# A per-token factor in a delta-rule scan: from a second copy of y on ACT to a copy of the keys on POOL

## The chip, the cores and the metric

One core of a Trainium2 chip runs the whole kernel in one launch. The metric is the device time of that core in microseconds, the median of several runs. The engines that matter here are PE (matrix products), DVE and ACT (vector work that may read the matrix products' memory, PSUM), POOL (vector work that reads and writes SBUF only) and SP, which issues the DMAs. Each engine works through its own queue in order; an instruction that must wait holds up everything behind it on its engine.

## What is computed

One encoder layer: a normalisation, one projection whose columns feed two head groups, and an output projection. Group B is windowed attention. Group A, where the change lies, is a gated delta rule, run forward and backward over the sequence, in chunks. The kernel uses chunks of 128 tokens where the reference uses 64. Cut to the step that is touched, the reference is:

```python
def step(state, inp):
    q_i, k_i, u_i, w_i, g_i, a_i = inp
    v_new = u_i - jnp.einsum('bhcd,bhde->bhce', w_i, state)
    o = (jnp.einsum('bhcd,bhde->bhce', q_i * jnp.exp(g_i)[..., None], state)
         + jnp.einsum('bhcs,bhse->bhce', a_i, v_new))
    g_last = g_i[..., -1]
    k_dec = k_i * jnp.exp(g_last[..., None] - g_i)[..., None]
    state = state * jnp.exp(g_last)[..., None, None] + jnp.einsum('bhcd,bhce->bhde', k_dec, v_new)
    return state, o
```

The state product sums over the tokens of a chunk. The factor exp(g_last - g) belongs to a token, so it may stand on the keys (as above) or on v_new: the sum is the same.

## The kernel before

Four heads, 16 chunks of 128 tokens each, two directions. From about 775 us on, the four heads' scans follow each other. Inside `scan(h, H)` a loop runs over 16 steps and, in each, over the two directions d; their states are independent of each other. One step and direction is: `pk` = the chunk's keys times the state (PE, L847); `r` from it on DVE (L849); `py` = the inverted triangular matrix times r (PE, L856); `yk` and `y`, two copies of py from PSUM to SBUF on ACT, the first with the per-token factor `ck` (L861, L863); the state product `po[:, 0]` of the keys `ks` and yk (PE, L865); the new state `S` on DVE (L868); and the outputs `po[:, 1]` and `po[:, 2]` (PE, L874, L858), which are put together in `oacc` on ACT and DVE (L881 to L885). The last step makes no new state, so 120 of the 128 chunk steps have a yk.

While head h is scanned, later heads are prepared. `pre_front` reads keys, queries and values, transposes them (`tr`, `trv`), squares and sums the keys on ACT (`jk`, L716, whose sums are `ssk`), adds the decay mask on POOL (`v_q` and `dc`, L699), takes a square root on POOL (`nk`, L718), scales the values by it on ACT (`vs`, L749) and makes the products `gh` (L728) and `ma` (L737). `solve` inverts small diagonal blocks on DVE, 31 columns one after the other (L775, L779). `invert` reads these back (`xc`, transposed `xt`), places them in `iv` and `ma` with copies on DVE and POOL (L802, L819) and builds the full inverse with products `pi` on PE (L807). As filling work PE also takes the attention group's share of the output projection, units of twelve products `pcs` (L622 to L624) with their splits `mhs` and `mls`. A unit takes a PSUM bank that `trv` or `gh` uses too, so it cannot begin before `vs` has read trv. At a scan's end `post` normalises and transposes the outputs (`jko`, `sso`, `tro`).

The order on each engine is not the program's. `set_order` builds the graph of dependencies with estimated durations, plans a queue for each engine, and then moves single instructions or short runs of them by a table of numbers, `TURNS`, one string for each engine.

Of the kernel before, what the change touches and what calls it, by code (L numbers as in the profile page):

```python
# [7 lines left out]
F32 = mybir.dt.float32  # L8
F32R = mybir.dt.float32r
AF = mybir.ActivationFunctionType  # L10
ALU = mybir.AluOpType
# [4 lines left out]
P = 128  # L16
# [556 lines left out]
def phase_b(ctx, wide, xe, ae, late, tc, t, ident, consts, hp, mix_dn, mix_sw, kq_d, v_d, zdn_d, zsw_d, dp, out):  # L573
# [259 lines left out]
    def scan(h, H):  # L833
# [3 lines left out]
        for i in range(NCH):  # L837
            for d in range(2):
# [20 lines left out]
                if i < NCH - 1:  # L859
                    yk = rp.tile([P, P], F32, tag="yk", name=f"yk{nm}", bufs=3)  # L860
                    A.activation(yk, py, AF.Copy, scale=ck[:, d, c : c + 1])  # L861
                y = rp.tile([P, P], F32, tag="y", name=f"y{nm}", bufs=3)
                A.activation(y, py, AF.Copy)  # L863
                if i < NCH - 1:
                    T.matmul(po[:, 0], ks[c4][:, cl], yk, start=True, stop=True)  # L865
                    s_new = rp.tile([P, P], F32, tag=f"S{d}", name=f"S{nm}", bufs=3)
                    if i:
                        V.scalar_tensor_tensor(  # L868
                            s_new, st[d], egt[:, d, c, h : h + 1], po[:, 0], ALU.mult, ALU.add
                        )  # L870
                    else:
                        V.tensor_copy(s_new, po[:, 0])
                    st[d] = s_new
# [185 lines left out]
    for c, e in zip(ORD[::2], ORD[1::2]):  # L1059
# [37 lines left out]
    ),  # L1097
    "DVE": (
# [455 lines left out]
```

## Time and profile before

| what | value |
|---|---|
| median of 3 runs | 1241.33 us (1239.07 to 1242.42) |
| the profiled execution | 1243.42 us, its span 1241.2 us |
| PE busy | 1206.3 us, 97% of the span |
| DVE busy | 945.5 us, 76% |
| ACT busy | 728.2 us, 59% |
| POOL busy | 524.5 us, 42% |
| chain that ended last | PE 82%, DVE 8%, DMA 4%, POOL 2%, ACT 2%, issue 2% |

The span runs from the first to the last instruction; 2.2 us of the profiled execution lie outside it. Matrix products overlap in their pipeline, so "busy" is an upper value of PE's work. Idle time of PE is what another order or a faster neighbour can give back.

### The profile page before, as it was taken

To read this page: it belongs to the slowest core of one execution; us is meant where nothing else is said; L and a number is where in the kernel's file an instruction comes from. 1 tells how busy PE (TensorE), PEld (TensorE's weight loads), DVE (VectorE), ACT (ScalarE), POOL (GpSimd) and SP (SyncE) were. 2 spreads that over 40 slices of the span, in tenths; PEclk is the share of its full clock that TensorE was granted. 3 is DMA by queue.
4 is the path that set the end of the run, shared out by engine and by line. 5 is a ranking of instruction groups with operands and counts; after the bars stand their busy time and mean duration, and the time that the engine had idled before them with its cause. 6 is when DMAs were issued, how large, how long until landed. Compare 5 with 4: busy or idle time off the path is not lost.

```text
span 1241.2 us, 22493 instructions
## 1 busy us (share of the span) xinstructions
PE 1206.3 (97%) x7080; PEld 1041.0 (84%) x7080; DVE 945.5 (76%) x2325; ACT 728.2 (59%) x2169; POOL 524.5 (42%) x845
## 2 busy tenths in 40 slices
PE   9999999999999999999999999899899899999998
PEld 9998888888889988887878877798689689888787
DVE  5523689999854369999997577799779989866765
ACT  6432476766634357776666546758566855686421
POOL 2243454754202185656532203704652461670442
PEclk9999999999999999999999999999899999999999
DMA  7653242523354434430115857967965875853785
GB/s 233 203 152 126 78 157 74 197 65 103 103 195 148 139 110 153 132 103 31 65 48 168 258 160 228 262 211 210 260 184 169 255 218 161 244 187 107 250 281 207
DMA packets 232295, 205.87 MB, mean 166 GB/s; under 512 B 49137, under 2 KB 181873, under 8 KB 232178
## 3 DMA queue, kind: packets, MB, share of 16 engines
q1 hardware_dynamic: 232178, 204.45, 53.4%
q8 instruction: 56, 0.92, 0.3%
q14 instruction: 61, 0.50, 0.1%
HBM read 139.32 MB, written 65.08 MB: 165 GB/s over the span
## 4 chain that ended last, share of the span: by engine, by line
PE 82%; DVE 8%; DMA 4%; POOL 2%; ACT 2%; issue 2%; SPq 0%; POOLq 0%; ACTq 0%; DVEq 0%
PE pf_c L224 7%; PE pf_c L223 7%; PE pf_c L225 7%; PE pf_z L223 4%; PE pf_z L224 4%; PE pf_z L225 4%; PE pi L807 4%; PE pt L416 3%; PE pq_q L238 2%; PE pq_q L237 2%; PE pq_q L236 2%; PE py L856 2%; PE pcd L1021 2%; PE pcd L1020 2%; PE pcd L1022 2%; PE pcs L622 2%
## 5 line engine op out<-in xcount | busy, mean ns | idle before, releaser
L223 PE MATMUL pf_c<-xhi,wh_c 128*128 128x512 f32 x384 | 155.0, 404 | 0.0
L224 PE MATMUL pf_c<-xlo,wh_c 128*128 128x512 f32 x384 | 154.4, 403 | 0.0
L225 PE MATMUL pf_c<-xhi,wl_c 128*128 128x512 f32 x384 | 153.9, 401 | 0.0
L295 DVE SCALAR_TENSOR_TENSOR acc<-pf_c,cw,acc 128x512 f32<-128x512 f32 (+1 forms) x192 | 141.1, 743 | 4.1 <-ACT acc L291 1.7
L411 POOL TENSOR_SCALAR pr<-pr,st 128x384 f32<-128x384 f32 (+1 forms) x128 | 76.4, 616 | 108.4 <-DVE st L409 72.8
L420 ACT ACTIVATE ph<-pt 128x512 fp32r<-128x512 f32 x92 | 53.1, 596 | 61.3 <-PE pt L416 54.4
L402 ACT ACTIVATE pr<-pr,st 128x384 f32<-128x384 f32 (+1 forms) x128 | 76.1, 596 | 16.0 <-DVE st L398 15.7
L225 PEld LDWEIGHTS pf_c<-xhi,wl_c 128*128 128x128 f32 x384 | 72.2, 188 | 13.2
L223 PEld LDWEIGHTS pf_c<-xhi,wh_c 128*128 128x128 f32 x384 | 72.4, 188 | 12.2
L224 PEld LDWEIGHTS pf_c<-xlo,wh_c 128*128 128x128 f32 x384 | 72.3, 188 | 12.1
L861 ACT ACTIVATE yk<-py,ck 128x128 f32<-128x128 f32 x120 | 44.0, 367 | 58.5 <-PE py L856 57.0
L398 DVE CUSTOM_DVE_ANT_0 pr<-s,mask,sink 128x384 f32<-128x384 f32 (+1 forms) x128 | 74.0, 595 | 3.6 <-PE pt L416 1.7
L237 PE MATMUL pq_q<-wh_q,xlo 128*128 128x256 f32 x256 | 72.1, 282 | 0.0
L238 PE MATMUL pq_q<-wl_q,xhi 128*128 128x256 f32 x256 | 71.9, 281 | 0.0
L236 PE MATMUL pq_q<-wh_q,xhi 128*128 128x256 f32 x256 | 71.4, 280 | 0.0
L416 PE MATMUL pt<-ident,pr 128*128 128x128 f32 x368 | 67.4, 273 | 1.1 <-DVE q L380 0.5
L718 POOL TENSOR_TENSOR nk<-ssk,pw 128x4 f32<-128x4 f32 x16 | 16.6, 1035 | 119.5 <-DVE ssk L717 119.5
L421 DVE TENSOR_TENSOR pl<-pt,ph 128x512 fp32r<-128x512 f32 x92 | 61.6, 683 | 6.0 <-ACT ph L420 5.4
L622 PE MATMUL pcs<-wohs,mhs 128*128 128x512 f32 x128 | 57.4, 449 | 5.4 <-ACT mhs L616 1.9
L416 PEld LDWEIGHTS pt<-ident,pr 128*128 128x128 f32 x368 | 48.1, 140 | 16.9 <-POOL pr L411 2.4
L623 PE MATMUL pcs<-wohs,mls 128*128 128x512 f32 x128 | 55.4, 433 | 0.5 <-DVE mls L617 0.5
L624 PE MATMUL pcs<-wols,mhs 128*128 128x512 f32 x128 | 54.3, 424 | 0.2 <-DVE wols L600 0.2
(336 smaller groups left out, 4017.3 us busy)
## 6 DMA issues: line engine op xcount, KB each, us to landing
kqc<-kq_d SPq DMA_DIRECT2D x120, 128.0 KB, 3.0
ws_c<-wt SPq DMA_DIRECT2D x48, 256.0 KB, 3.5
k_q<-kq_d SPq DMA_DIRECT2D x16, 512.0 KB, 5.1
mxs<-mix_sw SPq DMA_DIRECT2D x32, 256.0 KB, 3.3
xrs<-x SPq DMA_DIRECT2D x32, 256.0 KB, 3.6
part<-xrs SPq DMA_DIRECT2D x32, 256.0 KB, 2.5
xrd<-part SPq DMA_DIRECT2D x32, 256.0 KB, 3.5
out<-xrd SPq DMA_DIRECT2D x32, 256.0 KB, 2.3
```

What stands on the lines that cost most here:

```text
L223: T.matmul(ps, hi[:, k, cs], xhi[b][:, k], start=(k == 0), stop=False)
L224: T.matmul(ps, hi[:, k, cs], xlo[b][:, k], start=False, stop=False)
L225: T.matmul(ps, lo[:, k, cs], xhi[b][:, k], start=False, stop=(k == KC - 1))
L236: T.matmul(ps[:, :n], xh, hi[:, k, :n], start=(k == 0), stop=False)
L237: T.matmul(ps[:, :n], xl, hi[:, k, :n], start=False, stop=False)
L238: T.matmul(ps[:, :n], xh, lo[:, k, :n], start=False, stop=(k == KC - 1))
L295: V.scalar_tensor_tensor(av, ps[:, lo:], cw[:, i, k : k + 1], av, ALU.mult, ALU.add)
L398: V.tensor_tensor_reduce(pr[j][:, :n], ps[:, :n], mask[:, lo * P : hi * P], 1.0, sink[:, hh : hh + 1], ALU.add, ALU.min, accum_out=nm[:, j ...
L402: A.activation(pr[j][:, :n], pr[j][:, :n], AF.Exp, bias=nm[:, j : j + 1], scale=-1.0, accum_out=den[:, j : j + 1])
L411: G.tensor_scalar(pr[j][:, :n], pr[j][:, :n], den[:, j : j + 1], 1.0, ALU.mult, ALU.mult)
L416: T.transpose(pt[:, j], pr[j][:, (kb - lo) * P : (kb - lo + 1) * P], ident)
L622: T.matmul(ps, mh[:, k], wh[:, k], start=(k == 0), stop=False)
```

## The change

The copy yk is gone. In its place POOL writes `kd`, the keys times the same factor ck, into a ring of three buffers, and the state product takes kd and the plain copy y. kd needs nothing that the running step makes: keys and factors are ready before the scan starts. Its buffer comes free when the state product three before it has read it.

```diff
@@ scan
                 if i < NCH - 1:
-                    yk = rp.tile([P, P], F32, tag="yk", name=f"yk{nm}", bufs=3)
-                    A.activation(yk, py, AF.Copy, scale=ck[:, d, c : c + 1])
+                    kd = rp.tile([P, P], F32, tag="yk", name=f"kd{nm}", bufs=3)
+                    G.tensor_scalar(kd, ks[c4][:, cl], ck[:, d, c : c + 1], None, ALU.mult)
                 y = rp.tile([P, P], F32, tag="y", name=f"y{nm}", bufs=3)
                 A.activation(y, py, AF.Copy)
                 if i < NCH - 1:
-                    T.matmul(po[:, 0], ks[c4][:, cl], yk, start=True, stop=True)
+                    T.matmul(po[:, 0], kd, y, start=True, stop=True)
@@ TURNS: all five strings are replaced, for example the end of Pool's
-        "1,2 1,4 -5 4,12 1 -2 1,5 1 -2 1 1 -2 1,5 1 -2 4 -4,3 1,13 1,4 -5 4,4"
+        "-3,2 1,37 1 -2 1,6 1 -2 1 4 -5,4 1,6"
```

The graph has other instructions now, so the planned queues differ as well as the table, on every engine and in every stage. Three places matter below. In a name such as yk1_0_2 the numbers are head, direction and step; in nk2 and v2_q the digit is the head and the buffer; dc2_3_1 is head 2, quarter 3; the last number is the tile's own.

On ACT, at the start of head 1's scan, the queue was:

```order
L816 ACTIVATE b11_1_10511<-pi0_1_1_10506 128x512
L861 ACTIVATE yk1_0_0_10688<-py1_0_0_10685,ck1_9822 128x128
L863 ACTIVATE y1_0_0_10690<-py1_0_0_10685 128x128
L736 ACTIVATE v2_q_7777<-v2_q_7777,ngc_4962 128x128
L861 ACTIVATE yk1_1_0_10701<-py1_1_0_10698,ck1_9822 128x128
L863 ACTIVATE y1_1_0_10703<-py1_1_0_10698 128x128
```

With the change the same place reads:

```order
L863 ACTIVATE y1_0_0_10690<-py1_0_0_10685 128x128
L816 ACTIVATE b11_1_10511<-pi0_1_1_10506 128x512
L863 ACTIVATE y1_1_0_10703<-py1_1_0_10698 128x128
L879 ACTIVATE oacc1_0_10696<-po1_0_0_10686 128x128
L879 ACTIVATE oacc1_3_10709<-po1_1_0_10699 128x128
L863 ACTIVATE y1_0_1_10723<-py1_0_1_10717 128x128
L736 ACTIVATE v2_q_7777<-v2_q_7777,ngc_4962 128x128 x3
```

Two rows of yk are gone, and the decay mask's exponentials (L736, on v2_q) stand behind the third y where one stood between the first and the second pair.

On POOL, at the end of head 0's scan, the last quarter of head 2's preparation stood so before:

```order
L699 TENSOR_TENSOR v2_q_7777<-v2_q_7777,dmask_4923 128x512 x2
L718 TENSOR_TENSOR nk2_11396<-ssk2_11395,pw_4931 128x4
L795 TENSOR_TENSOR g1_1_10492<-xhi_h_9090 128x512
L699 TENSOR_TENSOR v2_q_7777<-v2_q_7777,dmask_4923 128x512
L718 TENSOR_TENSOR nk2_11396<-ssk2_11395,pw_4931 128x4
L699 TENSOR_TENSOR dc2_3_1_11627<-dc2_3_1_11627,dmask_4923 128x512
L613 TENSOR_TENSOR mxs9_0_11722<-mxs9_0_11722,zcs9_0_11724 128x512
```

and now so, with the first copies of head 1's keys among it:

```order
L699 TENSOR_TENSOR v2_q_7777<-v2_q_7777,dmask_4923 128x512 x2
L613 TENSOR_TENSOR mxs9_0_11722<-mxs9_0_11722,zcs9_0_11724 128x512
L718 TENSOR_TENSOR nk2_11396<-ssk2_11395,pw_4931 128x4
L861 TENSOR_SCALAR kd0_1_14_9732<-ks0_0_7947,ck0_7806 128x128
L861 TENSOR_SCALAR kd1_0_0_10688<-ks1_0_9978,ck1_9822 128x128
L861 TENSOR_SCALAR kd1_1_0_10701<-ks1_3_10051,ck1_9822 128x128
L861 TENSOR_SCALAR kd1_0_1_10721<-ks1_0_9978,ck1_9822 128x128
L718 TENSOR_TENSOR nk2_11396<-ssk2_11395,pw_4931 128x4
L699 TENSOR_TENSOR v2_q_7777<-v2_q_7777,dmask_4923 128x512
L699 TENSOR_TENSOR dc2_3_1_11627<-dc2_3_1_11627,dmask_4923 128x512
```

The last nk2 stood behind a v2_q row before and stands ahead of it now; four kd rows are ahead of it.

On POOL, at the end of head 1's scan, the rows of head 3's preparation were:

```order
L718 TENSOR_TENSOR nk3_12986<-ssk3_12985,pw_4931 128x4
L699 TENSOR_TENSOR v2_q_7777<-v2_q_7777,dmask_4923 128x512 x2
L718 TENSOR_TENSOR nk3_12986<-ssk3_12985,pw_4931 128x4 x2
L699 TENSOR_TENSOR v2_q_7777<-v2_q_7777,dmask_4923 128x512
L819 COPY ma2_0_11553<-xt2_0_0_12008 32x4x32 x2
```

and are now:

```order
L699 TENSOR_TENSOR v2_q_7777<-v2_q_7777,dmask_4923 128x512 x2
L718 TENSOR_TENSOR nk3_12986<-ssk3_12985,pw_4931 128x4
L861 TENSOR_SCALAR kd2_0_0_12278<-ks2_0_11562,ck2_11399 128x128
L861 TENSOR_SCALAR kd2_1_0_12291<-ks2_3_11635,ck2_11399 128x128
L861 TENSOR_SCALAR kd2_0_1_12311<-ks2_0_11562,ck2_11399 128x128
L699 TENSOR_TENSOR v2_q_7777<-v2_q_7777,dmask_4923 128x512
L718 TENSOR_TENSOR nk3_12986<-ssk3_12985,pw_4931 128x4
L699 TENSOR_TENSOR dc3_3_1_13212<-dc3_3_1_13212,dmask_4923 128x512
```

Here the last nk3 stood ahead of the third v2_q row and now stands behind it and behind three kd rows.

## Rows read from the trace of the kernel before

**Rows 1.** The page, parts 1 and 2: PE busy; its granted clock in 40 slices (tenths).

```profile
PE 1206.3 (97%) x7080; PEld 1041.0 (84%) x7080; DVE 945.5 (76%) x2325; ACT 728.2 (59%) x2169; POOL 524.5 (42%) x845
PEclk9999999999999999999999999999899999999999
```

**Rows 2.** Stretches: length, busy PE, PEld, DVE, ACT, POOL (instructions), clock, DMA share, GB/s.

```profile
868.00:899.00 31.00, 24.82 (x129) 21.00 (x129) 22.48 (x67) 17.78 (x74) 17.96 (x37) 0.83 0.90 255
961.00:992.00 31.00, 25.37 (x161) 20.88 (x161) 28.00 (x95) 27.75 (x136) 11.90 (x16) 1.00 0.89 262
775.00:1155.00 380.00, 356.59 (x2473) 318.91 (x2472) 313.65 (x949) 258.29 (x959) 164.83 (x287) 0.99 0.70 206
```

**Rows 3.** Waits of PE, 775 to 1155: total us, times, longest us.

```profile
PE po L865 <- ACT yk L861: 1.9, 4, 1.2
PE pcs L622 <- ACT mhs L616: 1.9, 2, 1.2
PE pcs L622 <- ACT vs L749: 1.9, 1, 1.9
...
PE trv L745 <- ACT jk L716: 1.6, 3, 0.8
PE pcs L622 <- ACT wohs L599: 1.5, 2, 0.9
```

**Rows 4.** Groups of ACT, 775 to 1155: count, busy us, mean ns, idle before.

```profile
L861 ACT ACTIVATE yk<-py,ck 128x128 f32<-128x128 f32 x120 | 44.0, 367 | 58.5 <-PE py L856 57.0
L863 ACT ACTIVATE y<-py 128x128 f32<-128x128 f32 x127 | 34.6, 272 | 1.8 <-PE py L856 1.7
```

**Rows 5.** Two POOL operations by line: ns least/median/most, shapes.

```profile
L109 POOL TENSOR_SCALAR sink<-sink x1: 259/259/259, 27.9 to 27.9; 128x8 f32<-128x8 f32 x1
L411 POOL TENSOR_SCALAR pr<-pr,st x128: 472/589/1616, 143.6 to 663.8; 128x384 f32<-128x384 f32 x112, 128x256 f32<-128x256 f32 x16
```

**Rows 6.** Timeline of ACT, start of head 1's scan: start, us, row, [idle before].

```profile
902.52 0.40 ACT L736 ACTIVATE v_q<-v_q,ngc 128x128 f32<-128x128 f32 x1 [1.98 <-POOL v_q L699]
902.83 0.35 ACT L861 ACTIVATE yk<-py,ck 128x128 f32<-128x128 f32 x1
```

**Rows 7.** Timeline of PE at the same place.

```profile
903.23 0.49 PE L865 MATMUL po<-yk,ks 128*128 128x128 f32 x2 [1.22 <-ACT yk L861]
```

**Rows 8.** Timeline of POOL at the end of head 0's scan.

```profile
873.21 1.27 POOL L699 TENSOR_TENSOR v_q<-v_q,dmask 128x512 f32<-128x512 f32 x1 [6.86 <-DMA v_q<-gr_d]
874.43 1.02 POOL L718 TENSOR_TENSOR nk<-ssk,pw 128x4 f32<-128x4 f32 x1
```

**Rows 9.** Timeline of PE at the same place, into head 1's inversion.

```profile
876.68 0.50 PE L622 MATMUL pcs<-wohs,mhs 128*128 128x512 f32 x1 [1.87 <-ACT vs L749]
...
884.17 1.91 PE L807 MATMUL pi<-iv,g 128*128 128x128 f32 x8 [2.00 <-DVE iv L802]
```

**Rows 10.** Stretches at the same place, columns as in the stretches above.

```profile
876.00:882.00 6.00, 5.32 (x16) 4.07 (x16) 3.52 (x11) 4.72 (x21) 3.99 (x10) 0.72 1.01 275
882.00:886.00 4.00, 2.00 (x9) 1.64 (x8) 3.80 (x16) 1.20 (x9) 0.73 (x2) 0.79 1.05 296
886.00:892.00 6.00, 5.31 (x25) 4.88 (x25) 4.17 (x14) 3.69 (x11) 4.34 (x12) 0.57 0.75 212
```

**Rows 11.** Timeline of POOL at the end of head 1's scan.

```profile
982.77 1.01 POOL L718 TENSOR_TENSOR nk<-ssk,pw 128x4 f32<-128x4 f32 x1 [5.38 <-DVE ssk L717]
983.74 1.27 POOL L699 TENSOR_TENSOR v_q<-v_q,dmask 128x512 f32<-128x512 f32 x1
```

**Rows 12.** Timeline of POOL and DVE inside head 0's scan.

```profile
844.06 1.28 POOL L613 TENSOR_TENSOR mxs<-mxs,zcs 128x512 f32<-128x512 f32 x1
...
844.62 0.95 DVE L779 TENSOR_TENSOR X<-X,tm 128x207 f32<-128x207 f32 x1
```

**Rows 13.** Groups of DVE, 775 to 1155: the two products of the solve.

```profile
L775 DVE TENSOR_TENSOR tm<-L,X 128x31 f32<-128x31 f32 (+15 forms) x93 | 34.2, 368 | 2.3 <-POOL X L770 1.4
L779 DVE TENSOR_TENSOR X<-X,tm 128x31 f32<-128x31 f32 (+15 forms) x93 | 34.0, 365 | 0.7
```

138 rows, old and new, of the table TURNS are left out of this document.

## Prediction, made before the changed kernel ran

> **What bounds the kernel now.** I read the page first, for where engines are busy and where PE's clock falls. PE is busy 97% of the span, and its granted clock is full in every slice but one, near 880 us [rows 1]. So the kernel is worth about what PE must do, and a change can win only where PE stands still or runs at the lower clock. The view of busy time by stretch then says where that is. In the scans, 775 to 1155 us, PE is busy 356.6 of 380 us, so it is idle for 23.4; 6.2 of these lie in 868 to 899 and 5.6 in 961 to 992, which are the ends of head 0's and head 1's scans [rows 2]. The change touches no instruction outside the scans except by order, so these 23.4 us are the field.
>
> Next, who ends PE's waits there [rows 3]. ACT is named for most of what is shown: 1.9 us for yk, 1.9 for vs, and 5.0 for mhs, jk and wohs together. The reader should see two things. The wait that the change attacks by name is small. And one of its four cases, 1.22 us [rows 7], is not made by yk at all: ACT stood 1.98 us on the decay mask from POOL, with yk queued behind it [rows 6].
>
> Last, the two stretches with the idle time. At the end of head 0's scan POOL waits 6.86 us for a DMA and only then adds the mask, and nk stands behind that row, without idle time of its own [rows 8]. nk feeds vs on ACT, and PE waits 1.87 us for vs; later it waits 2.00 us for DVE's copies into iv [rows 9]. After the first of these idles the granted clock is 0.72 over 876 to 882, 0.79 over 882 to 886 and 0.57 over 886 to 892 [rows 10]: it goes between the full 2.4 GHz and 1.2 GHz. The price is 6 x 0.28 = 1.7, 4 x 0.21 = 0.8 and 6 x 0.43 = 2.6 us, together 5.1.
>
> **The change, part by part.**
>
> *yk leaves ACT.* 120 activations at 367 ns, 44.0 us [rows 4]. PE has no fewer products and none of another shape, so nothing falls off PE. For the state product the data is ready after y at 272 ns instead of after yk at 367, so 0.1 us earlier in each step, and the output product, which waited for yk and y one after the other, has it earlier by yk's whole 367 ns. What this is worth is bounded by the 1.9 us of PE's waits for yk above and by nothing below. I take all of it: 1.22 us of it are the case in which the exponentials stood ahead of yk, and in the new ACT queue they stand behind the first three y, and the three other cases share 0.7, of which 0.1 each is sure. **-1.9.**
>
> *The room on ACT.* ACT is busy 258.3 of 380 us in the scans [rows 2] and will be busy about 214: from 68% to 56%, a sixth less. PE's other waits for ACT that a shorter queue could cut are the 5.0 us of mhs, jk and wohs [rows 3]. Bounds 0 and 5.0; nearest to the lower, because these waits are for work that is itself fed late, so I cut them by the same sixth. **-0.9.**
>
> *kd comes to POOL.* No such row exists. The same operation took 259 ns on 8 columns and 472 at the least, 589 at the median, on 384 [rows 5]; on the straight line between, 128 columns cost 259 + (213 to 330) x 120/376 = 327 to 364 ns. 120 of them are 39 to 44 us, so POOL is busy some 206 of the 380 us where it was 165 [rows 2]. POOL has the room, and kd needs nothing of its step. What hides it is that it may run up to three products ahead. The cover is gone where a kd stands behind a row that waits, or three kd rows of the next head stand in front of preparation at a boundary: there are three boundaries, 3 x 0.36 = 1.1 us at each, so 0 to 3.2. At the end of head 0's scan the 6.86 us in which POOL waited cover it. I take half a microsecond for places that I can't see. **+0.5.**
>
> *kd against DVE.* A product of the solve that began while POOL ran a row of 1.28 us took 0.95 us [rows 12] where such products take 0.37 on average [rows 13]; it ended 0.2 us after POOL did. So a POOL row can hold up DVE. The Trainium skill, SBUF — State Buffer, Who interferes with whom, has it as a rule: a DVE instruction with two SBUF inputs contends with a GpSimd instruction that reads SBUF, and the later one blocks until the first is done. The trace's 0.95 us agrees, and by that rule each kd is such an instruction, which speaks against the change. By rows: kd covers 41 of 380 us, 11%; of the 186 products of the solve some 20 would start inside a kd and lose half of 0.34 us each, 3.4 us of DVE. DVE is idle 66 of the 380 us [rows 2], and that is what I let hide it; with that cover gone the 3.4 us come back, as the solve ends before the inversion can begin. **0, bound +3.4.**
>
> *The order at the end of head 0's scan.* nk now stands ahead of the row that waited for the DMA. If its input is ready, vs comes earlier by up to the row that stood before it, and PE's 1.87 us [rows 9] go. Without that idle I expect the first fall of the clock, 1.7 us, to go too. The 2.00 us for iv stay, as the copies wait on a DMA that reads the solve back, and with them the later 3.4 us at the lower clock. Bounds: 0, if the idle only moves to the copies of iv, and 1.9 + 5.1 = 7.0. **-3.6.**
>
> *The order at the end of head 1's scan.* The other way round: the fourth nk stood ahead of the third mask row and now stands behind it and three kd rows. In the trace before, nk waited 5.38 us there for its own input and the mask took 1.27 us right after it [rows 11]. If the mask runs in that gap nothing is lost; if it begins just as the input arrives, 1.3. **+0.6**, half.
>
> Elsewhere PE hardly stands still and I count the new order as nothing, within the 2 us by which three runs differ. The sum is -1.9 - 0.9 + 0.5 + 0 - 3.6 + 0.6 = -5.3. The profiled execution took 1243.4 us, 2.2 of them outside its span, so the same execution would take 1238.1. It was 2.1 above the median of the runs, 1241.3; against the median I predict **1236.0 us**.
>
> **Rivals.**
>
> *Nothing to gain.* The idle time at the boundaries hangs on the DMA and the solve, and merely changes its name; then only yk's 1.9 us are left, and half a microsecond of kd is paid: 1241.3 - 1.4 = 1239.9. For it speaks that PE's 2.00 us for iv, the longest wait of rows 9, has no ACT and no nk in it. Against it: ACT stands behind every wait of rows 3.
>
> *DVE held by kd.* The lock of rows 12 falls on the solve while it is on the path: 1236.0 + 3.4 = 1239.4. It decides from the point where DVE's 66 us of idle time do not lie where the solve runs.
>
> *Slower: POOL ties the boundary to the scan.* A kd of the next head can't be written before the state product three before it has read its buffer, and POOL's queue is in order, so nk, the mask and the copies into iv behind it wait for the last products of the scan. Then PE meets at each of two further boundaries what it met at the first, 1.9 us of waiting and 1.7 at the lower clock, 7.2 in all, against 1.9 gained: 1241.3 + 5.3 = 1246.6. It decides as soon as head 0's last state product ends later than nk's input; that nk had no idle time before [rows 8] only says that the input was there by then.
>
> *More than forecast.* The second fall of the clock goes as well, 3.4 us: about 1232, and with all of ACT's 5.0 us 1228.
>
> **How the numbers follow.** 0.3% of the time, 3.7 us, is about what a measurement of this kernel can tell from no change; faster is below 1237.6 and slower above 1245.1. Chances: the forecast, 1231 to 1237.6, 0.40; more than it 0.10; nothing to gain 0.17; DVE held 0.09; slower 0.24. So faster 0.50, same 0.26, slower 0.24. The likeliest case by itself spans 1231 to 1240. All gains at their bounds give 1241.3 - 1.9 - 5.0 - 7.0 = 1227.4, all costs with no gain 1241.3 + 3.2 + 3.4 + 1.3 = 1249.2; the range is 1227 to 1249, which leaves out about one in eight.
>
> **What the profile will show.** ACT busy 44 us less, near 684, and POOL about 41 more, near 565. kd at 327 to 364 ns in 120 rows. PE's wait for yk replaced by one for y of under 1 us. In the stretch at the end of head 0's scan PE idle under 4 us where it was 6.2, the wait for vs gone, and the clock above 0.83. DVE's two solve products still near 0.37 us on average; above 0.40 the lock is at work. Wrong would be: PE or its weight loads waiting for kd on POOL by more than 2 us in total, POOL waiting for PE ahead of nk, or a fall of the clock at another boundary. And if the time moves by more than 3 us while the scans, 775 to 1155, keep their length, it was the order in other stages and not the change.

## The result, and the profile after

The changed kernel takes 1248.86 us (median of 7 runs, 1246.82 to 1253.69) against 1241.33 of the kernel before (7 runs, 1239.07 to 1244.80): ratio 1.0066, 95% interval 1.0045 to 1.0086. It is slower by some 8 us where 5 us of gain were predicted. The profiled execution took 1251.24 us, 1249.5 of them its span.

The page of the changed kernel, parts 1 and 2, answers [rows 1]:

```profile
PE 1206.7 (97%) x7080; PEld 1035.9 (83%) x7080; DVE 950.8 (76%) x2325; ACT 698.1 (56%) x2049; POOL 604.9 (48%) x965
...
PEclk9999999999999999999999999999999999999999
```

TensorE (PE) has the same 7080 products and the same busy time, so the 8 us are time in which it stands still. ACT has 30 us less where 44 were expected, because a yk row and the y row behind it overlapped by some 0.1 us (829.62 + 0.37 against 829.88 in the rows under e7). POOL has 80 more where 41 were expected. The operation on POOL says why, in the view by tile of kd (least, median and most ns; then what POOL waited for ahead of it, and who waited for kd: us, times):

```profile
L861 POOL TENSOR_SCALAR kd<-ks,ck x90: 592/603/1442, 773.6 to 1141.9; 128x128 f32<-128x128 f32 x90
L861 POOL TENSOR_SCALAR kd<-xlo_h,ck x30: 593/606/1466, 913.5 to 1157.2; 128x128 f32<-128x128 f32 x30
...
  PE po L865: 49.1, 35
...
  PEld po L865: 1.9, 3
  PE po L865: 0.9, 2
```

A kd takes 603 ns and not 327 to 364. PE's products wait 0.9 us in all for a kd and its weight loads 1.9, together just over the 2 us that the prediction named as a sign against it. So the price is real, but little of it is paid at the state product. Where is it? I cut the span at the copies that begin a head's scan and at its last S, and asked for the stretches. Of the kernel before, head 0's scan and all four scans, then the stretches from one scan to the next and their sum (columns as in [rows 2]):

```profile
788.50:869.20 80.70, 77.80 (x553) 71.16 (x552) 68.73 (x215) 59.04 (x227) 26.67 (x40) 1.00 0.75 222
...
sum 289.10, PE 281.20 PEld 255.83 DVE 243.53 ACT 197.09 POOL 103.08; mean PE 70.30 PEld 63.96 DVE 60.88 ACT 49.27 POOL 25.77
...
869.20:901.00 31.80, 25.60 (x132) 21.32 (x130) 21.75 (x66) 17.61 (x72) 19.70 (x43) 0.84 0.92 264
976.90:1005.80 28.90, 24.26 (x145) 19.71 (x145) 25.32 (x77) 20.86 (x84) 18.10 (x42) 1.00 0.81 228
...
sum 75.80, PE 63.60 PEld 53.11 DVE 56.76 ACT 50.42 POOL 51.58; mean PE 21.20 PEld 17.70 DVE 18.92 ACT 16.81 POOL 17.19
```

And of the changed kernel:

```profile
788.40:876.00 87.60, 81.11 (x553) 71.63 (x552) 75.84 (x217) 53.66 (x202) 48.70 (x78) 1.00 0.75 225
...
sum 302.20, PE 284.99 PEld 255.83 DVE 253.03 ACT 173.74 POOL 186.27; mean PE 71.25 PEld 63.96 DVE 63.26 ACT 43.44 POOL 46.57
...
876.00:902.90 26.90, 21.95 (x130) 17.82 (x129) 22.83 (x66) 16.92 (x71) 18.16 (x39) 1.00 0.97 270
980.70:1011.90 31.20, 26.91 (x152) 22.77 (x153) 24.96 (x79) 19.38 (x77) 17.61 (x37) 0.95 0.94 251
...
sum 71.30, PE 61.44 PEld 51.74 DVE 55.21 ACT 45.28 POOL 47.83; mean PE 20.48 PEld 17.25 DVE 18.40 ACT 15.09 POOL 15.94
```

The ends of the scans, where I looked for the gain, give it: 4.5 us less in sum, and at the end of head 0's scan the clock stays at 1.00. The scans, where I counted the new order as nothing, cost 13.1 us. Head 0's has the same 553 products and takes 6.9 us longer; PE's idle time in the scans goes from 289.1 - 281.2 = 7.9 to 302.2 - 285.0 = 17.2 us. The waits of PE in 775 to 1163, as in [rows 3], name the engine:

```profile
PE gh L728 <- DVE ma L737: 3.4, 5, 0.9
PE po L874 <- DVE S L868: 2.8, 6, 0.9
PE pcs L623 <- DVE mls L617: 2.6, 3, 1.5
PE pcs L622 <- ACT mhs L616: 2.6, 3, 1.5
PE pk L847 <- DVE S L868: 2.4, 3, 1.2
...
PE po L865 <- ACT y L863: 1.2, 3, 0.4
```

Summed over the whole view, 775 to the end of the scans, ACT is named for 10.8 us before and 8.1 after, as hoped; DVE for 9.0 before and 18.7 after. The view of before begins with two lines that [rows 3] leaves out, and both name DVE:

```profile
PE pi L807 <- DVE iv L802: 4.3, 2, 2.3
PE gh L728 <- DVE ma L737: 2.0, 3, 1.1
```

So DVE stood behind nearly as much of PE's waiting as ACT before the change, and the rows from which the prediction was worked out don't say so.

A last reading is worked out from the records of both traces. A step of the scan is a loop: S, product pk, row r on DVE, product py, y on ACT, product po, the next S. For 28 steps of each of the four heads I took the time from the end of one link to the start of the next, for every run of interest (mean us of 112; each direction goes through 56 of them one after the other, so 0.1 us is 5.6 us of scan):

```
               S>pk  pk>r  r>py  py>y  y>po  po>S   loop
before         0.61  0.28  0.66  0.53  0.49  0.31   5.04
after          0.81  0.38  0.62  0.28  0.66  0.35   5.27
e1             0.59  0.33  0.67  0.36  0.78  0.34   5.24
e3             0.82  0.38  0.61  0.26  0.65  0.33   5.20
e5             0.61  0.28  0.71  0.33  0.77  0.31   5.20
e7             0.63  0.28  0.68  0.42  0.68  0.27   5.13
e13            0.57  0.44  0.85  0.27  0.67  0.32   5.28
e14            0.55  0.61  0.66  0.26  0.65  0.30   5.21
e15            0.39  0.43  0.77  0.56  0.50  0.31   5.13
e17            0.62  0.29  0.64  0.31  0.76  0.28   5.06
e18            0.85  0.36  0.65  0.32  0.63  0.33   5.30
```

Before to after: 0.23 x 56 = 12.9 us, the 13.1 of the stretches. y starts 0.25 us earlier, as the change wants. 0.17 of it is gone by the start of po, and 0.30 are lost at S>pk and pk>r, links that the change doesn't touch, except by order. S>pk goes with the order, whoever makes the factor: 0.59 to 0.63 in the runs of the table with the order of before, 0.81 to 0.85 with the new one, but for e13 to e15, which move pk.

### The profile page after: what moved, and what is told of

Same layout as the page of the kernel before. It is cut to its first block, busy times and chain, and to the rows that moved or that the text cites. A ratio compares the mean times of both kernels' runs of the same rounds, so it can differ in the third digit from the quotient of the medians.

```text
span 1249.5 us, 22576 instructions
## 1 busy us (share of the span) xinstructions
PE 1206.7 (97%) x7080; PEld 1035.9 (83%) x7080; DVE 950.8 (76%) x2325; ACT 698.1 (56%) x2049; POOL 604.9 (48%) x965
## 4 chain that ended last, share of the span: by engine, by line
PE 71%; DVE 11%; DMA 7%; POOL 4%; issue 3%; ACT 2%; SPq 0%; POOLq 0%; DVEq 0%; ACTq 0%
PE pf_c L224 6%; PE pf_c L225 6%; PE pf_c L223 6%; PE pf_z L223 3%; PE pf_z L224 3%; PE pf_z L225 3%; PE pt L416 3%; PE pi L807 2%; PE pq_q L238 2%; PE pq_q L237 2%; PE pq_q L236 2%; DMA zs<-wt 2%; PE pcd L1020 2%; PE pcd L1021 2%; PE pcd L1022 2%
## 5 line engine op out<-in xcount | busy, mean ns | idle before, releaser
L861 POOL TENSOR_SCALAR kd<-ks,ck 128x128 f32<-128x128 f32 x90 | 60.2, 673 | 41.2 <-PE po L865 37.1
L863 ACT ACTIVATE y<-py 128x128 f32<-128x128 f32 x128 | 35.0, 274 | 66.8 <-PE py L856 65.4
L330 POOL TENSOR_TENSOR t1q<-ql,tabq 128x512 f32<-128x512 f32 x16 | 22.3, 1394 | 67.5 <-DMA ql<-q_d 38.3
```

## Experiments

Three theories. **A, price:** kd on POOL costs 0.60 us, in a queue with other work behind it. **B, order:** the new order of the queues costs, whoever makes the factor. **C, ring:** a kd waits for one of three buffers, and POOL's queue waits with it. Where a run sets rows by hand, the queues stand in it as written lists in place of planner and table. Each ratio is to the kernel before, run on the same chip. The runs lie on several chips, so two of them are compared by their ratios and not by their times; the difference of two ratios is uncertain by 0.002 to 0.003.

| run | order | factor made by | us | ratio | 95% interval |
|---|---|---|---|---|---|
| changed kernel | new | kd, POOL, 0.60 us, 3 buffers | 1248.86 | 1.0066 | 1.0045 to 1.0086 |
| e1 | before | kd, POOL, 0.60, 3 | 1258.12 | 1.0125 | 1.0103 to 1.0146 |
| e2 | new | yk, ACT | 1259.54 | 1.0129 | 1.0109 to 1.0148 |
| e3 | new | kd, POOL, 0.375, 3 | 1246.37 | 1.0029 | 1.0016 to 1.0042 |
| e4 | new | kd, POOL, 0.60, 5 | 1255.63 | 1.0101 | 1.0082 to 1.0119 |
| e5 | before | kd, POOL, 0.375, 3 | 1251.63 | 1.0085 | 1.0061 to 1.0110 |
| e6 | before, one pair of rows | yk, ACT | 1242.71 | 1.0005 | 0.9988 to 1.0023 |
| e7 | before | kd, ACT, at yk's place | 1247.09 | 1.0050 | 1.0033 to 1.0067 |
| e8 | e6's pair | as e7 | 1247.41 | 1.0051 | 1.0033 to 1.0068 |
| e9 | planner's | yk, ACT | 1261.86 | 1.0170 | 1.0135 to 1.0206 |
| e10 | planner's | kd, POOL, 0.60, 3 | 1287.59 | 1.0371 | 1.0346 to 1.0395 |
| e11 | planner's | kd, POOL, 0.375, 3 | 1280.36 | 1.0316 | 1.0291 to 1.0340 |
| e12 | new | kd, POOL, 0.375, 5 | 1244.49 | 1.0036 | 1.0018 to 1.0055 |
| e13 | new, pk and r earlier | as e3 | 1248.52 | 1.0046 | 1.0034 to 1.0058 |
| e14 | new, pk earlier | as e3 | 1247.00 | 1.0034 | 1.0022 to 1.0046 |
| e15 | before, pk earlier | yk, ACT | 1245.07 | 1.0028 | 1.0018 to 1.0038 |
| e16 | before | kd, POOL, 0.375, 5 | 1252.89 | 1.0065 | 1.0049 to 1.0081 |
| e17 | before, kd behind the y before | kd, ACT | 1245.05 | 1.0010 | 1.0000 to 1.0021 |
| e18 | new, kd behind the y before | kd, ACT | 1255.09 | 1.0094 | 1.0078 to 1.0110 |

### e1 and e2: operation and order exchanged

e1 has the change's code for kd in the queues of before; a place of POOL's queue, against before:

```diff
+L861 TENSOR_SCALAR kd_0_0_9111<-ks_0_7947,ck_7806 128x128
+L802 COPY iv_0_8813<-xt_0_2_8957 32x4x32
+L861 TENSOR_SCALAR kd_1_0_9124<-ks_3_8010,ck_7806 128x128
 L802 COPY iv_0_8813<-xt_0_2_8957 32x4x32
```

e2 has yk back in ACT's queue of the changed kernel:

```diff
+L861 ACTIVATE yk_0_0_9111<-py_0_0_9108,ck_7806 128x128
 L863 ACTIVATE y_0_0_9113<-py_0_0_9108 128x128
```

Expected of e1:

> The queues of TensorE, VectorE, SyncE and ScalarE stand as in the kernel before (ScalarE without the 120 yk), and the 120 kd are put into GpSimd's queue where a kd buffer comes free; nothing is left out. Theory A, the product on GpSimd is what costs (0.60 us each, over 80 us of GpSimd's time in its queue): the time is clearly above before, 1245 to 1252 us, with kd again near 600 ns. Theory B, the new order of the queues costs and the product as such does not: 1239 to 1243 us, as before. Theory C, the ring of three kd buffers holds up GpSimd's queue: as A, 1245 us or more, with GpSimd waiting over 40 us for TensorE ahead of kd.

Expected of e2:

> The queues stand as in the changed kernel, but ScalarE makes yk again, right ahead of each y, and GpSimd makes no kd; nothing is left out. Theory A (the product on GpSimd costs): most of the 7.5 us come back, 1240 to 1244 us, GpSimd near 525 us of busy time. Theory B (the new order costs): it stays at 1247 to 1251 us, or goes above it, since ScalarE has its 44 us of yk back in an order that was not made for it. Theory C (the ring of three): as A, 1240 to 1244 us.

Both are slower than both kernels: 1.0125 and 1.0129. A expected e1, which went beyond its range, and C's sign is there too: POOL waited 95.8 us for PE ahead of kd. B expected e2. None of the three explains both. Each operation does best in the order that belongs to it. e2 also has a stall that the changed kernel hasn't: ACT stands for a DMA with the next yk queued behind it. In the timeline of ACT in e2:

```profile
1070.08 0.63 ACT L984 ACTIVATE wod<-wos 128x512 fp32r<-128x512 f32 x1 [3.96 <-DMA wos<-wout]
```

So e2 doesn't price the order cleanly; e18 comes closer later.

### e3, e5, e11 and e12: the price of a kd

```diff
-G.tensor_scalar(kd, ks[c4][:, cl], ck[:, d, c : c + 1], None, ALU.mult)
+G.tensor_scalar(kd, ks[c4][:, cl], ck[:, d, c : c + 1], 1.0, ALU.mult, ALU.mult)
```

Expected of e3, in the new order:

> The changed kernel with its order; kd alone is written with a second multiplication, by 1.0, in the same instruction, the form in which the other products of GpSimd with a column stand in this kernel (472 to 589 ns for 384 columns). Theory A1, kd is slow by its form with one operation: kd falls from 0.60 to 0.30 to 0.37 us, GpSimd's busy time by about 30 us to 575, and 3 to 7 us of the loss come back, 1242 to 1246 us. Theory A2, kd is slow by something else (its operands, or VectorE working beside it): kd stays at 0.60 us and the time at 1247 to 1251 us. Theory B (the order): kd may fall, and the time stays at 1247 to 1251 us.

The view by tile of kd in e3:

```profile
L861 POOL TENSOR_SCALAR kd<-ks,ck x90: 364/375/1220, 773.5 to 1138.5; 128x128 f32<-128x128 f32 x90
L861 POOL TENSOR_SCALAR kd<-xlo_h,ck x30: 364/376/1237, 914.4 to 1153.9; 128x128 f32<-128x128 f32 x30
```

The same product with one more operation in it takes 375 ns in place of 603, and the time falls to 1246.4, just above what A1 gave. Of the two rows that I had priced kd by, [rows 5], the products of 384 columns have two operations; the one of 8 columns has one.

Expected of e5, e1 with this line:

> As e1 (the queues of the kernel before, kd put into GpSimd's queue where its buffer comes free), with kd written with a second multiplication by 1.0; nothing is left out. Theory A (the price of kd, 0.60 us against 0.375 in this form): of the 14.7 us that e1 lost against before most come back, 1243 to 1249 us. Theory C (GpSimd's queue is tied to TensorE's products wherever kd stands in an order that was not made for it, 96 us of waits in e1): at most 4 us come back, 1253 to 1258 us.

The ratio goes from 1.0125 to 1.0085: 5 us of e1's 15 come back, close to C's 4 and far from A's most.

Expected of e12, e4 (below) with this line:

> e4 with kd of two operations: the changed kernel's order, five kd buffers, 0.375 us per kd. Theory A (price): 4 to 7 us less than e4, 1247 to 1252 us, near e3, as the buffers don't matter. Theory C (with a fast kd the ring of three is what is left): clearly below e3, under 1243 us. If five buffers cost something of their own, as e4 against the changed kernel suggests, it stays 2 us or more above e3.

It fell to e3's level, as A said. With e10 to e11 below the faster form is worth 0.0037, 0.0040, 0.0065 and 0.0055 of 1243 us in four settings, 5 to 8 us. So A holds for about half of what the changed kernel loses, 0.0037 of 0.0066, and the intervals leave room on either side. In the new order with the fast form 0.3% stay.

### e4 and e16: the ring

```diff
-kd = rp.tile([P, P], F32, tag="yk", name=f"kd{nm}", bufs=3)
+kd = rp.tile([P, P], F32, tag="yk", name=f"kd{nm}", bufs=5)
```

Expected of e4, the changed kernel:

> The changed kernel with its order, and five buffers for kd instead of three (five are what fits in SBUF), so that kd may be made up to two more chunks ahead of its product. Theory A (the price of kd): it stays within 2 us of the changed kernel, 1247 to 1251 us, with kd at 0.60 us. Theory C (GpSimd's queue stands behind TensorE's products, 49 us of waits ahead of kd): these waits fall to under 15 us and the time comes down by 4 us or more, to 1245 us or less. Theory B (the order): 1247 to 1251 us.

Expected of e16, e5:

> e5 (before's queues, kd of two operations on GpSimd where a buffer of three came free) with five buffers for kd in the same queues; nothing is left out. Theory C, the ring ties GpSimd's queue to TensorE's products (110 us of waits ahead of kd in e5): the waits fall under 40 us and most of e5's 10 us come back, 1241 to 1245 us. Theory without C: kd's buffers don't matter for what TensorE waits for, within 3 us of e5, 1249 to 1254 us.

In e4 POOL's waits for PE ahead of kd, from the view by tile, are as small as C asked:

```profile
  PE po L865: 13.3, 11
```

The time got no better, 1.0101 against 1.0066; with the fast kd e12 stands level with e3. In e16 the waits fall from 109.9 to 43.9 us, and the ratio from 1.0085 to 1.0065, inside the intervals. POOL waiting for its buffers is no cause; C falls. Why e4 is slower than the changed kernel stays open; their intervals overlap by a little.

### e6 and e8: the rows at the end of head 0's scan

e6, POOL's queue against before (e8 has this and e7's line):

```diff
+L718 TENSOR_TENSOR nk_11396<-ssk_11395,pw 128x4
 L699 TENSOR_TENSOR v_q<-v_q,dmask 128x512
-L718 TENSOR_TENSOR nk_11396<-ssk_11395,pw 128x4
```

Expected:

> The kernel before with its operations (yk on ScalarE) and one pair of rows of GpSimd's queue exchanged: at the end of head 0's scan the third square root nk stands ahead of the mask row that waits 6.86 us for a DMA, as in the changed kernel; nothing is left out. Theory of the prediction: vs comes some 1.2 us earlier or more, TensorE's 1.87 us for vs and the first fall of the clock go, 1236 to 1240 us against 1243.5 of before on this chip. Rival: the idle time only moves to the copies of iv, 1242 to 1245 us.

1.0005: nothing. The view of stretches of e6, as [rows 10], and its timeline of PE:

```profile
876.00:882.00 6.00, 2.12 (x10) 1.45 (x8) 3.22 (x12) 3.35 (x17) 2.42 (x7) 0.94 0.95 257
882.00:886.00 4.00, 2.56 (x10) 2.30 (x11) 3.79 (x14) 0.61 (x2) 2.57 (x4) 0.50 0.92 242
886.00:892.00 6.00, 6.00 (x28) 5.64 (x27) 4.11 (x15) 3.08 (x10) 3.26 (x12) 0.54 0.98 264
...
882.75 2.05 PE L807 MATMUL pi<-iv,g 128*128 128x128 f32 x8 [4.62 <-DVE iv L802]
```

The wait of 1.87 us for vs [rows 9] is gone, and the one for iv has grown from 2.00 to 4.62. The clock falls later and costs as much: 6 x 0.06 + 4 x 0.50 + 6 x 0.46 = 5.1 us, as before. In the changed kernel the same rows and the same products stand so:

```profile
886.00:892.00 6.00, 4.14 (x24) 2.91 (x24) 5.50 (x18) 3.30 (x11) 3.49 (x11) 1.00 0.83 229
...
888.80 1.16 PE L807 MATMUL pi<-iv,g 128*128 128x128 f32 x8 [0.75 <-DVE iv L802]
```

There PE reaches this product 4.6 us later than in the kernel before, after a scan that ended 6.8 us later, and iv is nearly ready. Nk alone doesn't win the shorter stretch. That it is what a late scan leaves of a wait that runs beside it fits these rows, but no run shows it by itself.

Expected of e8:

> The two edits before together: kd on ScalarE at yk's place, and nk ahead of the mask row on GpSimd. If both gain and add up, 1233 to 1239 us; if the end of head 0's scan is bound by something that either edit frees alone, as the better one of the two, 1238 to 1241 us.

1.0051, as e7 alone; the pair adds nothing there either.

### e7 and e17: the same algebra without POOL

```diff
-G.tensor_scalar(kd, ks[c4][:, cl], ck[:, d, c : c + 1], None, ALU.mult)
+A.activation(kd, ks[c4][:, cl], AF.Copy, scale=ck[:, d, c : c + 1])
```

Expected of e7, in yk's place:

> The kernel before with its queues, and kd in place of yk made by ScalarE at yk's place in its queue, so that ScalarE's count of instructions is the same and GpSimd gets none; the state product takes kd and y as in the changed kernel; nothing is left out. Theory A (GpSimd's price is what the change loses by, the algebra is harmless): not above before, and y comes right behind py because kd is made while ScalarE waits for py: 1238 to 1243 us. Theory B (making the factor ahead of py is itself worth nothing, since S hangs on other work): 1242 to 1245 us, as before on this chip. If the state product with kd costs something that yk did not (kd's buffer is held longer, its weight load comes late), it goes above 1246 us.

1.0050, where A wanted no loss; the time is that of the last branch, a price of kd itself at the state product, which e17 below speaks against. Where ACT comes late to a step, kd now stands between py and y. A step of the kernel before, in ACT's timeline:

```profile
829.62 0.37 ACT L861 ACTIVATE yk<-py,ck 128x128 f32<-128x128 f32 x1
829.88 0.27 ACT L863 ACTIVATE y<-py 128x128 f32<-128x128 f32 x1
```

and of e7:

```profile
830.45 0.39 ACT L861 ACTIVATE kd<-ks,ck 128x128 f32<-128x128 f32 x1
830.75 0.27 ACT L863 ACTIVATE y<-py 128x128 f32<-128x128 f32 x1
```

The state product has its data 0.37 us after ACT begins in the one, 0.57 in the other. e17 moves kd out of the way; its queue of ACT, against before:

```diff
+L861 ACTIVATE kd_1_0_9124<-ks_3_8010,ck_7806 128x128
 L822 ACTIVATE iv_0_8815<-pi_0_1_8926 32x4x32
-L861 ACTIVATE yk_1_0_9124<-py_1_0_9121,ck_7806 128x128
 L863 ACTIVATE y_1_0_9126<-py_1_0_9121 128x128
```

Expected:

> e7 (before's queues, kd made by ScalarE) with 117 of the 120 kd moved up in ScalarE's queue to right behind the y before, three to four rows earlier, so that a kd never stands between py and its own y; nothing is left out. If e7 lost its 6 us because ScalarE, where it comes late to a step, does kd before y (y begins 0.42 us behind py on average, and 0.28 in the changed kernel): y comes as early as in the changed kernel and the time falls to 1239 to 1244 us. If ScalarE's rows behind the moved kd matter as much (output rows, copies of the inversion, mhs): 1245 to 1249 us, as e7.

1.0010: level with before, or a hair above. This is the cleanest look at what the change hoped for. y starts 0.22 us earlier on average, and po does not: py>y, y itself (0.27) and y>po are 1.29 us before and 1.35 in e17. In the kernel before po took yk, which ACT made first, so its data was ready nearly as early.

### e9 to e11: the planner's own queues

```diff
-TURNS = {
...
+TURNS = {e: "" for e in ("PE","DVE","Activation","Pool","SP")}
```

Expected of e9, yk:

> The kernel before with an empty table of moves, so that the queues are the planner's own; nothing is left out. It serves as the base of the next two: the table's worth is not known, and I expect 1255 to 1300 us.

Expected of e10, kd:

> The changed kernel with an empty table of moves: the planner sets the queues by its own rules in both, so this and the run before differ by the operation and what the planner makes of it, not by a search. Theory A (the price of kd on GpSimd, 0.60 us where the planner's cost formula says 190 + 1.02 x 128 = 321 ns): slower than with yk by 4 to 12 us. Theory B (the operation is harmless, the searched order is what loses): within 4 us of the run with yk, or faster, since ScalarE has 44 us less.

Expected of e11, kd of two operations:

> The run before with the second multiplication by 1.0 in kd, 0.375 us in place of 0.60, in the same queues. Theory A: 3 to 8 us less than the run before. Theory B: within 2 us of it.

With the same rules and no table kd on POOL is 25 us slower than yk on ACT (1.0371 to 1.0170), 18 us with the fast form. Theory A's sign; its size is larger, and more than kd's price, so the plan that follows the operation costs too. The table of moves is worth 21 us to the kernel before and 38 to the changed one.

### e13 to e15: two links of the loop

e13 and e14 move 59 products pk up in PE's queue, one of them here, and e13 also 24 rows r on DVE; e15 does the same with 65 pk in the order of before:

```diff
+L847 MATMUL pk_0_1_9136<-S_0_0_9116,kqc_0_1_9134 128x128
 L807 MATMUL pi_0_1_8926<-b_1_8916,iv_1_8814 128x128
 L807 MATMUL pi_0_1_8933<-iv_1_8814,b_1_8916 128x128
 L874 MATMUL po_0_0_9109<-y_0_0_9113,ma_0_7939 128x128
 L622 MATMUL pcs_0_10138<-wohs_10112,mhs_0_10132 128x512
-L847 MATMUL pk_0_1_9136<-S_0_0_9116,kqc_0_1_9134 128x128
```

Expected of e13:

> e3 (kd of two operations in the changed kernel's order) with 83 rows moved up in two queues: 59 products pk on TensorE and 24 rows r on VectorE, each as far as the rows in front of it began only after its input was ready, past filling work alone (pcs, pi, transposes, solve products, output rows). Nothing is left out. Theory B, the new order delays the scan's loop (S to pk 0.82 us against 0.61 before, pk to r 0.38 against 0.28, by the traces): both links fall back to 0.6 and 0.3 us, the loop from 5.20 to 4.9 to 5.1 us, and 1237 to 1243 us. Rival, TensorE is full and the filling work only comes later, at the ends of the scans: the loop gets shorter and the stretches between the scans longer, 1243 to 1247 us, as e3. If the delayed filling feeds others too late, it goes above 1248 us.

Expected of e14:

> e3 with the 59 products pk moved up on TensorE alone, VectorE's queue as it was. Theory B: S to pk falls to 0.6 us, some two thirds of what the run with both gains, 1239 to 1244 us. Rival: as e3, 1243 to 1247 us.

Expected of e15:

> The kernel before with the same rule applied to its own queue of TensorE: 65 products pk moved up past filling work. If the links of the loop are what the time hangs on, S to pk falls from 0.61 to under 0.5 us, the loop from 5.04 to 4.9 to 5.0, and 1234 to 1240 us. Rival, in an order in which TensorE is idle for 8 us in all the scans nothing is left to gain: 1240 to 1245 us.

None gained: 1.0046, 1.0034, 1.0028. The table of links shows it working and failing: S>pk fell to 0.55 in e14 and pk>r rose from 0.38 to 0.61; in e13, with r earlier as well, r>py rose to 0.85. What one link gives the next takes, in both orders. So the loss is seen at these links, but moving their rows doesn't win it back; which rows make it is not shown.

### e18: the new order with kd on ACT

ACT's queue, against the changed kernel, with e7's line:

```diff
+L861 ACTIVATE kd_0_1_9144<-ks_0_7947,ck_7806 128x128
 L822 ACTIVATE iv_0_8815<-pi_0_1_8926 32x4x32 x2
```

Expected:

> The changed kernel's queues, and kd made by ScalarE right behind the y before, as in e17, where that stood level with before; GpSimd makes no kd, no wait for a DMA is moved as in e2, and nothing is left out. The two runs differ by the order alone. Theory B (the searched order itself costs, with whatever makes the factor): 1247 to 1252 us, 3 to 7 us above before on this chip, with S to pk at 0.8 us and VectorE named for some 15 us of TensorE's waits. Rival (the order costs nothing and all of the loss is kd on GpSimd, also at 0.375 us): 1242 to 1246 us.

1.0094, 11.7 us above before where B gave 3 to 7, with POOL free of kd. The waits of PE, 775 to 1160, have the names of the changed kernel's:

```profile
PE gh L728 <- DVE ma L737: 3.1, 4, 0.9
PE py L856 <- DVE r L849: 2.9, 4, 1.6
PE po L874 <- DVE S L868: 2.7, 5, 1.6
```

DVE is named for 16.8 us in all; in e17, the same operation in the old order, for 10.2. One wait for a DMA is in it all the same, at the row that held e2 up, with a y behind it that PE waits for (ACT, then PE):

```profile
1066.15 0.63 ACT L984 ACTIVATE wod<-wos 128x512 fp32r<-128x512 f32 x1 [2.13 <-DMA wos<-wout]
...
1067.13 0.49 PE L856 MATMUL py<-r,ma 128*128 128x128 f32 x2 [1.58 <-ACT y L863]
```

So up to 1.6 us of e18's loss may be this wait. With e5, e3 and e17 the two edits can be crossed. The last two columns are the sums of the stretches of the scans and of those between them, cut as above in one profiled execution of each:

| order | kd made by | run | ratio | scans, us | between, us |
|---|---|---|---|---|---|
| before | ACT | e17 | 1.0010 | 290.6 | 75.7 |
| new | ACT | e18 | 1.0094 | 304.6 | 70.7 |
| before | POOL, 0.375 | e5 | 1.0085 | 298.2 | 75.7 |
| new | POOL, 0.375 | e3 | 1.0029 | 299.1 | 71.1 |

The new order costs 10.4 us where ACT makes kd (0.0084 of 1243) and gives 7.0 back where POOL does (0.0056). In the same way kd's move from ACT to POOL costs 9.3 us in the old order and gives 8.1 back in the new one. So neither has a price of its own. Between the scans the new order saves 5.0 and 4.6 us, whoever makes kd; inside them it costs 14.0 or 0.9. What adds up by either way is the algebra, +1.2 us (e17), the order and POOL together, +2.4 (e3 less e17), and the slow form, +4.6 (changed kernel less e3): 8.2.

## Why the prediction was wrong

*The step that failed* is the sentence "Elsewhere PE hardly stands still and I count the new order as nothing", together with the +0.5 for kd, a term of its own beside it. The sum has -1.9 - 0.9 + 0.5 = -2.3 us for the scans, and they came out 13.1 longer. The two terms don't add. The order costs 14.0 us of scan where ACT makes kd (e18 against e17) and 0.9 where POOL does (e3 against e5); kd on POOL costs 7.6 in the old order even at 0.375 us (e5 against e17), and the slow form 3.1 more (302.2 against e3's 299.1). That PE was idle for 7.9 us in the scans only says that little was left to win; it says nothing of what another order or a busier POOL can lose.

*kd comes to POOL, +0.5.* Mis-sized: 603 ns against 327 to 364. The longer of the two rows it was priced by has two operations; in that form kd takes 375 ns (e3), close to the forecast. The slow form alone costs 4.6 us here. Nor was it covered as I thought: with the fast form in the old order the kernel is at 1.0085 (e5) and 1.0065 (e16), against 1.0010 with kd on ACT. Which rows behind kd on POOL make these 7 to 9 us in the old order is not settled; little of it is PE waiting for kd itself.

*yk leaves ACT, -1.9.* Near zero. PE's wait for yk [rows 3] gave way to one of 1.2 us for y; y comes 0.22 us earlier, and the product doesn't (e17).

*The room on ACT, -0.9.* Right in sign for the changed kernel, whose waits of PE for ACT fell from 10.8 to 8.1 us. It hangs on the order: in the new one kd on POOL and not on ACT is worth 8.1 us (e3 against e18), in the old one it is a loss (e16 and e5 against e17).

*kd against DVE, 0, bound +3.4.* About right for the products themselves. The two products of the solve, in the groups of DVE, 775 to 1163, answer [rows 13]:

```profile
L775 DVE TENSOR_TENSOR tm<-L,X 128x31 f32<-128x31 f32 (+15 forms) x93 | 35.5, 382 | 5.5 <-POOL X L770 4.5
L779 DVE TENSOR_TENSOR X<-X,tm 128x31 f32<-128x31 f32 (+15 forms) x93 | 34.2, 367 | 0.9
```

93 x (14 + 2) ns = 1.5 us of DVE. The first line shows a cost that wasn't counted: DVE stood 4.5 us for POOL's clearing of X (L770), 1.4 before; whether that is on the path isn't shown. The lock shows on the other side: 25 of the 120 kd took over 0.7 us, up to 1.47. In the records of the trace each of the 25 overlaps a DVE row that reads two operands of SBUF or copies within it, and ends 0.38 to 0.48 us behind that row. That agrees with the Trainium skill, SBUF — State Buffer, Who interferes with whom, by which the later of the two engines stands until the other's instruction is done. Which is the later can't be told from the starts alone: 7 of the 25 began, by the records, up to 0.23 us ahead of the DVE row.

*The order at the end of head 0's scan, -3.6.* The stretch did become 4.9 us shorter and its clock stayed up, which looks like a hit. Most of it is the clock: PE's idle time there only went from 6.2 to 5.0 us. The stretches between the scans are shorter in every crossed run with the new order, so that gain goes with the order; but alone the rows named here give nothing (e6). The rival "nothing to gain" had this mechanism right, an idle time that changes its name.

*The order at the end of head 1's scan, +0.6.* That stretch grew by 2.3 us. PE's longest wait in it, 2.3 us, is for xhi_h on DVE, not for nk or vs, and the mask ran in the gap while nk still waited for its own input, so the step's mechanism is not what is seen:

```profile
984.62 1.27 POOL L699 TENSOR_TENSOR v_q<-v_q,dmask 128x512 f32<-128x512 f32 x1 [2.57 <-DMA v_q<-gr_d]
986.13 1.04 POOL L718 TENSOR_TENSOR nk<-ssk,pw 128x4 f32<-128x4 f32 x1 [0.24 <-DVE ssk L717]
```

*The rivals.* "Slower: POOL ties the boundary to the scan" gave 1246.6, near the result, for a wrong reason. At the end of head 0's scan POOL did wait for PE ahead of nk, as this rival has it (0.71 and 1.16 us), but nk then waited another 1.04 us for its own input from DVE:

```profile
874.31 0.60 POOL L861 TENSOR_SCALAR kd<-ks,ck 128x128 f32<-128x128 f32 x1 [0.71 <-PE po L865]
876.07 0.60 POOL L861 TENSOR_SCALAR kd<-ks,ck 128x128 f32<-128x128 f32 x1 [1.16 <-PE po L865]
877.72 1.04 POOL L718 TENSOR_TENSOR nk<-ssk,pw 128x4 f32<-128x4 f32 x1 [1.04 <-DVE ssk L717]
```

The stretches between the scans got shorter, and freeing POOL of its waits (e4, e16) won nothing that can be told from zero. Against "Nothing to gain" the prediction said that "ACT stands behind every wait of rows 3"; with the two lines for DVE that the rows leave out, this argument falls.

*Open:* which rows of the new order cost the scans their time when ACT makes kd, and which rows behind kd on POOL do in the old order. Moving pk and r (e13, e14) only moved the wait along the loop. No run beat the kernel before; e6 and e17 are level with it or just above.

## What to carry to other kernels

Price a moved operation by a row of the very same form on the new engine, operations per instruction included, and test the other form before searching an order around it. When a change comes with a new order, run all four: old and new operation, or a harmless variant of it, in old and new order. Here the order cost 10.4 us with one and gave 7.0 back with the other, so a single pair of runs would have named the wrong cause. Don't take a full engine as proof that the order there is free. A stretch that got shorter next to one that got longer is no gain until it is had alone.

## What was unexpected of the hardware

On POOL a product of 128x128 elements with a column takes 603 ns as an instruction with one operation and 375 ns with a second operation, a multiplication by 1.0, in the same kernel and order (medians of 90 each, the changed kernel and e3). With the first form POOL is busy 604.9 us, with the second 579.0.
